# Soft pauses for a background modulation stream, and the FFN's right columns first, in a two-layer diffusion trunk

## The chip, the cores and the metric

The kernel runs on one core of a Trainium2 chip, in one launch. The metric is the device time of that launch in microseconds (us). Engines are named as in the profile: PE (TensorE's matmuls) and PEld (its weight loads), DVE (VectorE), ACT (ScalarE), POOL (GpSimd) and SP (SyncE, which here only issues transfers).

## The reference, cut to what matters

Two layers with the same structure run over 640 tokens of width 1024: 128 context tokens and 512 latent tokens, each group with its own condition vector. Only the last part of a layer and its modulation matter here.

```python
def trunk_layer(x, cond, p, ctx):
    mod = jax.nn.silu(cond) @ p['w_mod'] + p['b_mod']          # 1024 -> 6 x 1024, fp32
    sh1, sc1, g1, sh2, sc2, g2 = [m[:, None, :] for m in jnp.split(mod, 6, axis=-1)]
    h = rms_norm(x, p['g_attn']) * (1 + sc1) + sh1
    a, new_ctx = mixer_sublayer(h, p, ctx)    # projection, three mixers, three branch products with gates, output product
    x = x + g1 * a
    h = rms_norm(x, p['g_ffn']) * (1 + sc2) + sh2
    x = x + g2 * conv_ffn(h, p)               # up 1024 -> 2 x 2816, width-3 convolution over tokens, a * silu(g), down
    return x, new_ctx
```

The modulation of a layer needs only the condition vectors, so layer 1's can be worked out at any time before layer 1 begins.

## The kernel before, in words

**The planner.** The kernel is written as Python generators ("streams"), and class Order interleaves them while the program is built. A stream yields the things that it waits for; `one` (L355) takes the first stream, by priority number, whose things are all there at the planner's own estimate of PE's time, and if none is, the one that is ready soonest. Each step then puts its instructions behind those already issued on their engines. On the chip nothing is reordered: each engine works through its list. Evacuations, weight preparation and factors have priority 0, most helpers 1, and the main stream, which issues the large products, 2. `later(ns)` (L324) is an event at PE's time plus ns; a stream that waits for it paces itself.

**Slots.** Nearly all intermediate tiles come from one pool of 49 slots in SBUF (tile `u`, NU = 49), which lends four more to the mixer. A stream that needs a slot waits until another gives one back. A second pool (`wb`) holds staged weights and their split halves.

**Products.** Weights and activations are split into a high and a low part, so a product with a 128x128 weight block is three matmuls (`mm3`, `product`). `proj_halves` (L692) makes the 640 columns as two halves of 320, each in a PSUM bank, one after the other, and waits for the activation's chunks two at a time. `proj_whole` (L708) makes both halves chunk by chunk in two banks.

**The FFN.** `ffn_steps` (L82) writes out the main stream's order. Two chunks of 128 hidden channels go in the plain way ("raw", tile `up`); they work on unnormalised input, so they can run while the norm is worked out. The other 20 are made by a seven-product scheme over halves of the depth and of the columns, a chunk being a `Pair` with the PSUM tiles pair_x, pair_y and pair_w. Its steps are "12" (products with B11 and B21), "67" (T2, T3), "54" (T1, T4) and "3" (B22). B11 and B21 are the right half of the columns of the normalised input; all others need the left half too. `modulate_factors` (L1006) makes the normalised, modulated input (tile `hv`) and starts `factors` (L931), which splits it and its sums into seven factors (tiles `f`, `f_hi`, `f_lo`) for each of four depth blocks: 28 slots that live through the whole FFN. Five parts of three to five chunks each are followed by eight down products (tile `dn`), woven between the later chunks; the activations of a part (`a_hi`, `a_lo`, two slots a chunk) are given back after its eighth.

**The modulation.** `Mod.rest` (L782) takes five slots, four of them a ring for weights and one for sums. It makes 1024 modulation values, a vector, in eight k-steps; a k-step loads two 256 KB transfers through SP's queue (tile `mod`) and has four small fp32 matmuls of 128x32 by 128x256, which work in four column groups of the array at once and are eight records in the profile. Two k-steps form a turn. Layer 0's last four vectors run early in the kernel with a pause of 4000 ns between turns. For layer 1's six vectors `next_mod` (L2285) waits for the event `calm`, which is set when layer 0's last branch product (tile `bb`) begins; it then has priority 3, behind the main stream, and no pause. `hurry` (L2292) waits for the FFN's first down product of part 1 (event `rush`), gives it priority 1 with a pause of 2000 ns.

Of the kernel before, what the change touches and what calls it, by code (L numbers as in the profile page):

```python
# [9 lines left out]
F32 = mybir.dt.float32  # L10
# [71 lines left out]
def ffn_steps():  # L82
# [5 lines left out]
    for n in range(NRAW, NFF + 1):  # L88
        up, last = n < NFF, n > NRAW
        weave += [("12", n)] * up + [("54", n - 1)] * last + [("67", n)] * up + [("3", n - 1)] * last  # L90
# [104 lines left out]
class Event:  # L195
    time = INF

# [67 lines left out]
class Order:  # L265
# [58 lines left out]
    def later(self, ns):  # L324

        return self.moment(self.at["PE"] + ns)

    def start(self, gen, prio):
        self.seq += 1
        self.streams.append([prio, self.seq, gen, ()])  # L330
        self.streams.sort(key=lambda s: s[:2])

    def lift(self, gen, prio):
        for s in self.streams:
            if s[2] is gen:
                s[0] = prio
        self.streams.sort(key=lambda s: s[:2])
# [17 lines left out]
    def one(self):  # L355
        now, best, at = self.at["PE"], None, INF
        for s in self.streams:
            r = max((self.ready(x) for x in s[3]), default=0.0)
            if r <= now:
                best = s  # L360
                break
            if r < at:
                best, at = s, r
# [15 lines left out]
def kernel(ctx: ExitStack, tc: tile.TileContext, I, O, depth=2):  # L379
# [360 lines left out]
    class Mod:  # L740
        def __init__(self, l, pc=None, ready=None):
            self.l, self.pc, self.ready, self.pause = l, pc, ready, 0.0 if l else 4000.0
# [39 lines left out]
        def rest(self, vectors, after, whole):  # L782
# [17 lines left out]
            for i in range(0, len(todo), 2):  # L800
                v, k0 = todo[i]
                yield ring[0] + ring[1] + [cT, od.later(self.pause)]
# [4 lines left out]
                for j in range(2):  # L807
                    for g in range(4):
                        mm(acc[32 * g:32 * g + 32, :256], cT[:, k0 + j, :], ring[j][g // 2][:, g % 2 * 256:g % 2 * 256 + 256],
                           k0 + j == a, k0 + j == b, tile_position=(0, 32 * g))  # L810
                if not whole or k0 == KC - 2:
# [6 lines left out]
                for j in range(2):  # L818
                    if i + 2 + j < len(todo):
                        yield [od.until(ring[j][1].ap)]  # L820
                        fetch(i + 2 + j)
                if k0 == KC - 2:
                    yield from self.finish(ms, (v * D,), 256, D)
# [107 lines left out]
    def factors(fa, fb, out, k):  # L931

        L, R = slice(0, HT), slice(HT, NT)
        h1, l1, h2, l2 = yield from ub.several("f_12", 4, 0, F32R)
        b11, b12, b21, b22 = fa[:, R], fa[:, L], fb[:, R], fb[:, L]

        def lo(nm, x, h, l):
            tt(l, x, h.bitcast(F32), SUB, sooner(HT))
            out[nm][k] = (h, l)
            out[nm].ready[k].time = od.known[l.tensor.name]  # L940

        yield [fa]
        act(h1[:, L], b11)
        yield [fb]
        act(h1[:, R], b21)
        act(h2[:, L], b22)
        yield [h1]
        lo("B11", b11, h1[:, L], l1[:, L])
        lo("B21", b21, h1[:, R], l1[:, R])
# [3 lines left out]
        yield [fb]  # L953
        tt(b22, b22, b12, SUB)
        tt(b12, b12, b11, SUB)
        tt(b11, b22, b11, ADD)
        tt(b21, b21, b11, SUB)
        yield [fa]
        act(h2[:, R], b12)
        h3 = yield from U("f_hi", F32R)  # L960
        act(h3[:, L], b11)
        yield [h2]
        lo("T1", b12, h2[:, R], l2[:, R])
        l3 = yield from U("f_lo", F32R)
        yield [h3]
        lo("T2", b11, h3[:, L], l3[:, L])
        act(h3[:, R], b21)
        h4 = yield from U("f_34", F32R)
        act(h4[:, L], b22)
        yield [h3]  # L970
        lo("T4", b21, h3[:, R], l3[:, R])
        yield [h4]
        lo("T3", b22, h4[:, L], h4[:, R])
        out.keep += [h1, l1, h2, l2, h3, l3, h4]
# [1146 lines left out]
    def ffn(l, x, raws, h, pc, mod, ss, nxt, nraws, rush):  # L2121
# [14 lines left out]
        for step in ffn_steps():  # L2136
# [13 lines left out]
            elif kind == "dn":  # L2150
                part, o = i, step[2]
                b0, nb = FFN_PARTS[part]
                if part == 1:
                    rush.time = 0.0
# [5 lines left out]
                yield from proj_halves(w, a, nb, finish(o, part), "dn")  # L2160
# [55 lines left out]
    def program():  # L2216
# [20 lines left out]
        for l in range(depth):  # L2237
# [5 lines left out]
            if l == 0:  # L2243
                od.start(mod.rest((2, 3, 4, 5), mod.have[3], False), 1)
# [3 lines left out]
            lazy = next_mod(nxt, calm)  # L2248
            od.start(lazy, 3)
# [27 lines left out]
            rush = Event()  # L2277
# [86 lines left out]
```

## Time and profile before

| | before |
|---|---|
| median of 3 runs (lowest, highest) | 2235.13 us (2232.56, 2236.04) |
| the profiled execution's own time | 2225.76 us |
| its span, first to last instruction | 2224.0 us |
| PE busy in the span | 2113.6 us (95%) |
| PEld, DVE, ACT, POOL busy | 1978.6, 1561.9, 1122.2, 212.6 us |
| mean granted TensorE clock | 0.989 |

The profiled execution is 9.37 us (0.42%) below the median of the runs. Times inside the trace are counted from the start of its span. Layer 0's FFN begins with the first `up` product at 646 us, layer 1's at 1767 us. A matmul's record is longer than the distance to the next one, since they are pipelined: a run of plain 128x320 matmuls at full clock starts one every 0.147 us or so, each being shown with about 0.31 us.

### The profile page before, as it was taken

The numbers are of one execution on the slowest core, as the hardware profiler recorded it, in microseconds if no ns is written. First come the engines' busy times: TensorE is split into PE (matmuls) and PEld (weight loads), VectorE is DVE, ScalarE is ACT, GpSimd is POOL, SyncE is SP. The second block draws the span as 40 slices with busy tenths as digits, with TensorE's granted clock in tenths as the row PEclk, the third lists the DMA queues.
The fourth block names the chain that finished last, engine by engine and source line by source line (L and its number), as shares of the span: only waits on it lengthen the run. The fifth ranks groups of instructions, "written<-read, shape, count | busy, mean of one in ns | idle before, by whom it ended". The sixth has DMA issues, their size and how long they took to land. (4 is left out here: it accounts for less than half of the span.)

```text
span 2224.0 us, 40076 instructions
## 1 busy us (share of the span) xinstructions
PE 2113.6 (95%) x16208; PEld 1978.6 (89%) x16208; DVE 1561.9 (70%) x2827; ACT 1122.2 (50%) x2063; POOL 212.6 (10%) x283
## 2 busy tenths in 40 slices
PE   6999999999998968999999999999999989999999
PEld 4878988899997826999998989888999988999999
DVE  5376679673579804978777876787745798687785
ACT  4355755553356402544556667455532575445452
POOL 0201010000120001010010110100001200100101
PEclk9999999999999989999999999999999999999999
DMA  9752221112324373222223112211114212232212
GB/s 307 258 182 76 69 64 50 39 48 69 112 81 152 112 246 107 90 78 94 77 65 133 62 54 70 72 51 39 39 57 133 76 39 68 76 98 71 95 65 91
DMA packets 85874, 209.33 MB, mean 94 GB/s; under 512 B 9590, under 2 KB 22518, under 8 KB 85688
## 3 DMA queue, kind: packets, MB, share of 16 engines
q1 hardware_dynamic: 84472, 204.66, 28.7%
q8 instruction: 128, 2.10, 0.4%
q0 software_dynamic: 1216, 2.10, 0.3%
q14 instruction: 58, 0.48, 0.1%
HBM read 197.81 MB, written 10.98 MB: 94 GB/s over the span
## 5 line engine op out<-in xcount | busy, mean ns | idle before, releaser
L454 ACT ACTIVATE w_h<-w_st 128x1024 fp32r<-128x1024 f32 (+4 forms) x292 | 273.7, 940 | 220.0 <-PE dn L445 57.5
L470 DVE TENSOR_TENSOR w_h<-w_st,w_h 128x1024 fp32r<-128x1024 f32 (+4 forms) x253 | 276.7, 1095 | 140.1 <-ACT w_h L454 133.9
L445 PE MATMUL dn<-a_hi,w_h 128*128 128x320 f32 x1408 | 321.4, 310 | 1.1 <-ACT a_hi L454 1.1
L445 PE MATMUL pair_x<-f,w_h 128*128 128x320 f32 x1440 | 230.1, 311 | 11.1 <-ACT f L454 5.7
L445 PEld LDWEIGHTS dn<-a_hi,w_h 128*128 128x128 f32 x1408 | 239.4, 189 | 1.3 <-ACT a_hi L454 1.3
L445 PEld LDWEIGHTS pair_x<-f,w_h 128*128 128x128 f32 x1440 | 216.1, 189 | 14.1 <-ACT f L454 5.9
L445 PE MATMUL dn<-a_lo,w_h 128*128 128x320 f32 x704 | 218.4, 310 | 2.6 <-DVE a_lo L470 2.6
L445 PEld LDWEIGHTS dn<-a_lo,w_h 128*128 128x128 f32 x704 | 133.2, 189 | 2.8 <-DVE a_lo L470 2.8
L482 DVE SCALAR_TENSOR_TENSOR x<-dn,modT,x 128x128 f32<-128x128 f32 (+2 forms) x240 | 97.2, 434 | 54.4 <-PE dn L445 54.1
L445 PE MATMUL gc<-h_hi,w_h 128*128 128x320 f32 x512 | 131.8, 324 | 2.1 <-ACT mg L454 2.1
L445 PE MATMUL ga<-h_hi,w_h 128*128 128x320 f32 x512 | 125.9, 316 | 0.0
L473 POOL TENSOR_TENSOR w_h<-w_st,w_h 128x1024 fp32r<-128x1024 f32 (+3 forms) x39 | 78.3, 2008 | 470.8 <-ACT w_h L454 308.4
L445 PE MATMUL gb<-h_hi,w_h 128*128 128x320 f32 x512 | 119.0, 312 | 0.0
L445 PE MATMUL wo<-m_hi,w_h 128*128 128x320 f32 x768 | 113.0, 309 | 0.0
L445 PEld LDWEIGHTS wo<-m_hi,w_h 128*128 128x128 f32 x768 | 112.8, 188 | 0.0
L445 PE MATMUL mod<-mod,cT 128*32 128x256 f32 x640 | 76.0, 412 | 31.1 <-DMA mod<-in_w_mod_dram 29.8
L445 PEld LDWEIGHTS gc<-h_hi,w_h 128*128 128x128 f32 x512 | 89.0, 189 | 9.5 <-ACT mg L454 3.1
L445 PEld LDWEIGHTS mod<-mod,cT 128*32 128x32 f32 x640 | 21.1, 111 | 78.2 <-DMA mod<-in_w_mod_dram 65.2
L445 PEld LDWEIGHTS ga<-h_hi,w_h 128*128 128x128 f32 x512 | 88.1, 188 | 2.4 <-issue 2.4
L454 ACT ACT_TABLE_LOAD x64 | 82.1, 1283 | 16.0 <-PE hss L445 11.1
L445 PEld LDWEIGHTS gb<-h_hi,w_h 128*128 128x128 f32 x512 | 86.8, 188 | 1.6 <-issue 1.4
L445 PE MATMUL pair_x<-f_hi,w_h 128*128 128x320 f32 x320 | 79.3, 316 | 5.7 <-ACT up_a L454 5.7
(414 smaller groups left out, 5350.4 us busy)
## 6 DMA issues: line engine op xcount, KB each, us to landing
w_st<-in_wt_dram SPq DMA_DIRECT2D x204, 512.0 KB, 3.4
mod<-in_w_mod_dram SPq DMA_DIRECT2D x160, 256.0 KB, 3.8
w_st<-in_wt_dram SPq DMA_DIRECT2D x48, 320.0 KB, 3.0
mod_w<-in_w_mod_dram SPq DMA_DIRECT2D x32, 256.0 KB, 6.4
xd<-x SPq DMA_DIRECT2D x16, 320.0 KB, 6.0
x<-xd SPq DMA_DIRECT2D x16, 320.0 KB, 3.2
w_st<-in_wt_dram SPq DMA_DIRECT2D x16, 256.0 KB
w_st<-in_wt_dram SPq DMA_DIRECT2D x16, 192.0 KB, 2.5
```

The costliest lines, as they stand in the source:

```text
L445: nc.tensor.matmul(out, lhsT, rhs, start=start, stop=stop, **kw)
L454: r = nc.scalar.activation(out=out, in_=in_, func=f, **kw)
L470: nc.vector.tensor_tensor(out, a, b, op=op)
L473: nc.gpsimd.tensor_tensor(out, a, b, op=op)
L482: nc.vector.scalar_tensor_tensor(out=out, in0=a, scalar=s, in1=b, op0=op0, op1=op1)
```

## The change

Three things change.

- **Soft pauses.** A pause becomes an event of a class of its own, `Soft`. `one` looks twice: with all events, and, if no stream is ready, once more without the soft ones. A pausing modulation stream is then taken although its pause is not over. `lift` and `hurry` are gone.
- **Layer 1's modulation** starts at the same event `calm`, but with priority 1 and a soft pause of 3000 ns, and a turn is one k-step, not two. Layer 0's last four vectors keep 4000 ns and two k-steps, softly.
- **The FFN.** The right columns of all eight depth blocks are normalised first and B11 and B21 made of them (`right_factors`), then the left columns and the other five factors (`left_factors`); all eight `hv` slots are held in between. The step "12" of the second chunk pair comes before "67" of the first. The first down product of each part is made by `proj_whole`.

```diff
     weave = []
-    for n in range(NRAW, NFF + 1):
-        up, last = n < NFF, n > NRAW
+    a, b = NRAW, NRAW + 1
+    weave += [("12", a), ("12", b), ("67", a), ("54", a), ("67", b), ("3", a)]
+    for n in range(NRAW + 2, NFF + 1):
+        up, last = n < NFF, True
         weave += [("12", n)] * up + [("54", n - 1)] * last + [("67", n)] * up + [("3", n - 1)] * last
...
+class Soft(Event):
+    pass
...
-    def later(self, ns):
-        return self.moment(self.at["PE"] + ns)
+    def later(self, ns, kind=Event):
+        e = kind()
+        e.time = self.at["PE"] + ns
+        return e
...
     def one(self):
-        now, best, at = self.at["PE"], None, INF
-        for s in self.streams:
-            r = max((self.ready(x) for x in s[3]), default=0.0)
-            if r <= now:
-                best = s
-                break
-            if r < at:
-                best, at = s, r
+        now = self.at["PE"]
+        for kinds in ((), Soft):
+            best, at = None, INF
+            for s in self.streams:
+                r = max((self.ready(x) for x in s[3] if not isinstance(x, kinds)), default=0.0)
+                if r <= now:
+                    return self.step(s)
+                if r < at:
+                    best, at = s, r
...
-        def rest(self, vectors, after, whole):
...
-            for i in range(0, len(todo), 2):
+            n = 1 if whole else 2
+            for i in range(0, len(todo), n):
                 v, k0 = todo[i]
-                yield ring[0] + ring[1] + [cT, od.later(self.pause)]
+                yield [t for j in range(n) for t in ring[(i + j) % 2]] + [cT, od.later(pause, Soft)]
                 if k0 == 0 or not whole:
...
-                for j in range(2):
+                for k in range(k0, k0 + n):
                     for g in range(4):
-                        mm(acc[32 * g:32 * g + 32, :256], cT[:, k0 + j, :], ring[j][g // 2][:, g % 2 * 256:g % 2 * 256 + 256],
-                           k0 + j == a, k0 + j == b, tile_position=(0, 32 * g))
+                        mm(acc[32 * g:32 * g + 32, :256], cT[:, k, :],
+                           ring[(i + k - k0) % 2][g // 2][:, g % 2 * 256:g % 2 * 256 + 256], k == a, k == b,
+                           tile_position=(0, 32 * g))
...
-    def factors(fa, fb, out, k):
-        L, R = slice(0, HT), slice(HT, NT)
-        h1, l1, h2, l2 = yield from ub.several("f_12", 4, 0, F32R)
+    L, R = slice(0, HT), slice(HT, NT)
+    def factor_lo(out, k, nm, x, h, l):
+        tt(l, x, h.bitcast(F32), SUB, sooner(HT))
+        out[nm][k] = (h, l)
+        out[nm].ready[k].time = od.known[l.tensor.name]
+    def right_factors(fa, fb, out, k):
+        h, l = yield from ub.several("f_12", 2, 0, F32R)
+        for nm, x, c in (("B11", fa, L), ("B21", fb, R)):
+            yield [x]
+            act(h[:, c], x[:, R])
+            yield [h]
+            factor_lo(out, k, nm, x[:, R], h[:, c], l[:, c])
+        out.keep += [h, l]
+    def left_factors(fa, fb, out, k):
         b11, b12, b21, b22 = fa[:, R], fa[:, L], fb[:, R], fb[:, L]
-        def lo(nm, x, h, l):
-            tt(l, x, h.bitcast(F32), SUB, sooner(HT))
-            out[nm][k] = (h, l)
-            out[nm].ready[k].time = od.known[l.tensor.name]
-        yield [fa]
-        act(h1[:, L], b11)
+        lo = lambda nm, x, h, l: factor_lo(out, k, nm, x, h, l)
+        h2, l2 = yield from ub.several("f_12", 2, 0, F32R)
         yield [fb]
-        act(h1[:, R], b21)
         act(h2[:, L], b22)
-        yield [h1]
-        lo("B11", b11, h1[:, L], l1[:, L])
-        lo("B21", b21, h1[:, R], l1[:, R])
         yield [h2]
         lo("B22", b22, h2[:, L], l2[:, L])
-        yield [fb]
+        yield [fa, fb, out["B11"].ready[k], out["B21"].ready[k]]
         tt(b22, b22, b12, SUB)
+        h4 = yield from U("f_34", F32R)
+        act(h4[:, L], b22)
         tt(b12, b12, b11, SUB)
         tt(b11, b22, b11, ADD)
-        tt(b21, b21, b11, SUB)
-        yield [fa]
-        act(h2[:, R], b12)
         h3 = yield from U("f_hi", F32R)
         act(h3[:, L], b11)
+        tt(b21, b21, b11, SUB)
+        l3 = yield from U("f_lo", F32R)
+        yield [h4]
+        lo("T3", b22, h4[:, L], h4[:, R])
+        yield [h3]
+        lo("T2", b11, h3[:, L], l3[:, L])
+        act(h2[:, R], b12)
+        act(h3[:, R], b21)
         yield [h2]
         lo("T1", b12, h2[:, R], l2[:, R])
-        l3 = yield from U("f_lo", F32R)
-        yield [h3]
-        lo("T2", b11, h3[:, L], l3[:, L])
-        act(h3[:, R], b21)
-        h4 = yield from U("f_34", F32R)
-        act(h4[:, L], b22)
         yield [h3]
         lo("T4", b21, h3[:, R], l3[:, R])
-        yield [h4]
-        lo("T3", b22, h4[:, L], h4[:, R])
-        out.keep += [h1, l1, h2, l2, h3, l3, h4]
+        out.keep += [h2, l2, h3, l3, h4]
...
     def modulate_factors(x, r, mod, i, offs, out):
         gsc, sh = mod.gsc[:, i], mod.T[:, 24 * i:24 * i + 8]
-        cols = [(slice(a, a + n), slice(offs[e], offs[e] + n), e) for e, (a, n) in enumerate(((0, NP), (NP, NS)))]
-        for k in range(KC // 2):
-            f = []
-            for kk in (k, k + KC // 2):
-                yield [r, mod.have[12 * i + 4 + kk // 2], mod.have[12 * i + kk // 2]]
-                v = yield from U("hv")
-                eng = sooner(NT)
-                for c, o, e in cols:
-                    tt(v[:, c], x[kk][:, c], r[:, o], MUL, eng)
-                yield [v]
-                for c, _, e in cols:
-                    act(v[:, c], v[:, c], AF.Identity, scale=gsc[:, kk, e:e + 1], bias=sh[:, kk, e:e + 1])
-                f.append(v)
-                del v
-            od.start(factors(f[0], f[1], out, k), 0)
-            del f
+        n = HT - NP
+        sides = (((slice(HT, NT), slice(offs[1] + n, offs[1] + NS), 1),),
+                 ((slice(0, NP), slice(offs[0], offs[0] + NP), 0), (slice(NP, HT), slice(offs[1], offs[1] + n), 1)))
+        v = [None] * KC
+        for cols, then in zip(sides, (right_factors, left_factors)):
+            for k in range(KC // 2):
+                for kk in (k, k + KC // 2):
+                    yield [r, mod.have[12 * i + 4 + kk // 2], mod.have[12 * i + kk // 2]]
+                    if v[kk] is None:
+                        v[kk] = yield from U("hv")
+                    eng = sooner(HT)
+                    for c, o, e in cols:
+                        tt(v[kk][:, c], x[kk][:, c], r[:, o], MUL, eng)
+                    yield [v[kk]]
+                    for c, _, e in cols:
+                        act(v[kk][:, c], v[kk][:, c], AF.Identity, scale=gsc[:, kk, e:e + 1], bias=sh[:, kk, e:e + 1])
+                od.start(then(v[k], v[k + KC // 2], out, k), 0)
+                if then is left_factors:
...
-                if part == 1:
-                    rush.time = 0.0
...
-                yield from proj_halves(w, a, nb, finish(o, part), "dn")
+                if o:
+                    yield from proj_halves(w, a, nb, finish(o, part), "dn")
+                else:
+                    ps, ev = (yield from proj_whole(w, a, nb, HT, "dn")), finish(o, part)
+                    for hf in range(2):
+                        od.start(ev(hf, ps.pop(0)), 0)
+                    del ps, ev
...
-                od.start(mod.rest((2, 3, 4, 5), mod.have[3], False), 1)
+                od.start(mod.rest((2, 3, 4, 5), mod.have[3], 4000.0, False), 1)
...
-            lazy = next_mod(nxt, calm)
-            od.start(lazy, 3)
+            od.start(next_mod(nxt, calm), 1)
...
-                od.start(hurry(nxt, lazy, rush), 1)
...
-            yield from nxt.rest(range(6), after, True)
+            yield from nxt.rest(range(6), after, 3000.0, True)
...
-    def hurry(mod, lazy, when):
-        yield [when]
-        mod.pause = 2000.0
-        od.lift(lazy, 1)
```

## Rows read from the trace of the kernel before

**Rows 1.** The page: PE's busy time, PE in 40 slices, GB/s in the slices
```profile
PE 2113.6 (95%) x16208; PEld 1978.6 (89%) x16208; DVE 1561.9 (70%) x2827; ACT 1122.2 (50%) x2063; POOL 212.6 (10%) x283
...
PE   6999999999998968999999999999999989999999
...
GB/s 307 258 182 76 69 64 50 39 48 69 112 81 152 112 246 107 90 78 94 77 65 133 62 54 70 72 51 39 39 57 133 76 39 68 76 98 71 95 65 91
```

**Rows 2.** Windows: stretch, length, busy of engines, clock, DMA share, GB/s
```profile
540.00:590.00 50.00, 50.00 (x343) 50.00 (x342) 28.36 (x40) 16.37 (x23) 6.18 (x4) 1.00 0.39 114
...
782.00:856.00 74.00, 47.11 (x291) 12.33 (x290) 3.55 (x24) 3.06 (x7) 3.57 (x5) 0.91 0.74 235
...
1797.00:1812.00 15.00, 6.11 (x26) 5.50 (x25) 14.51 (x30) 8.22 (x16) 0.20 (x2) 0.68 0.00 0
1812.00:1872.00 60.00, 55.11 (x363) 53.59 (x363) 58.83 (x99) 39.09 (x67) 0.41 (x4) 0.98 0.27 88
```

**Rows 3.** Timeline of PE: start, us, what, idle before with its releaser
```profile
782.68 1.07 PE L445 MATMUL mod<-mod,cT 128*32 128x256 f32 x16
...
855.48 0.42 PE L445 MATMUL pair_x<-f_hi,w_h 128*128 128x320 f32 x1 [0.70 <-ACT up_a L454]
```

**Rows 4.** Waits, 640 to 900: us in total, times, longest
```profile
POOL up_a L2069 <- PE mod L445: 72.9, 1, 72.9
...
PE mod L445 <- DMA mod<-in_w_mod_dram: 27.8, 39, 2.3
```

**Rows 5.** Timeline of SP's issues; tile mod's transfers, 640 to 900; tile bb
```profile
655.00 0.43 SPq L510 DMA_DIRECT2D pc<-in_prm_dram  x1
...
670.67 21.21 SPq L510 DMA_DIRECT2D mod<-in_w_mod_dram  x20
...
710.16 1.96 SPq L510 DMA_DIRECT2D mod<-in_w_mod_dram  x4
...
L510 SPq DMA_DIRECT2D mod<-in_w_mod_dram x96: 327/328/1172, 670.7 to 850.1; - x96
...
L445 PE MATMUL bb<-ob_hi,w_h x256: 302/309/313, 540.7 to 1710.8; 128*128 128x320 f32 x128
```

**Rows 6.** Timeline of PE: first pair in layer 0 and in layer 1
```profile
675.95 1.50 PE L445 MATMUL pair_x<-f,w_h 128*128 128x320 f32 x9
...
691.44 0.71 PE L445 MATMUL pair_x<-f,w_h 128*128 128x320 f32 x3
...
1796.79 1.48 PE L445 MATMUL pair_x<-f,w_h 128*128 128x320 f32 x9
1803.92 0.63 PE L445 MATMUL pair_x<-f,w_h 128*128 128x320 f32 x1 [5.65 <-ACT f L454]
1807.79 0.90 PE L445 MATMUL pair_x<-f,w_h 128*128 128x320 f32 x2 [3.24 <-DVE f L470]
...
1898.83 0.31 PE L445 MATMUL pair_x<-f_hi,w_h 128*128 128x320 f32 x1
```

**Rows 7.** Timeline of PE: modulation between other matmuls in layer 0
```profile
64.25 2.92 PE L445 MATMUL mod<-mod,cT 128*32 128x256 f32 x16 [1.98 <-DMA mod<-in_w_mod_dram]
...
82.87 0.30 PE L445 MATMUL rc<-h_hi,w_h 128*128 128x320 f32 x1
83.10 1.07 PE L445 MATMUL mod<-mod,cT 128*32 128x256 f32 x16
84.10 0.41 PE L445 MATMUL rc<-h_hi,w_h 128*128 128x320 f32 x1
...
85.09 0.38 PE L450 MATMUL modt<-cn,mod 128*128 128x128 f32 x2
```

**Rows 8.** DVE's groups, 1775 to 1815, shapes apart: busy, mean ns
```profile
L470 DVE TENSOR_TENSOR f<-hv,f 128x320 fp32r<-128x320 f32 x19 | 8.6, 487 | 0.0
...
L470 DVE TENSOR_TENSOR hv<-x,rstd 128x512 f32<-128x512 f32 x7 | 4.8, 685 | 0.2 <-ACT rstd L454 0.2
...
L470 DVE TENSOR_TENSOR hv<-x,rstd 128x128 f32<-128x128 f32 x7 | 2.3, 329 | 3.7 <-ACT rstd L454 3.7
```

**Rows 9.** Timeline of PE: first down product in layer 1
```profile
1868.52 0.41 PE L445 MATMUL dn<-a_hi,w_h 128*128 128x320 f32 x1 [1.05 <-ACT a_hi L454]
1871.54 0.63 PE L445 MATMUL dn<-a_lo,w_h 128*128 128x320 f32 x1 [2.61 <-DVE a_lo L470]
```

More of the change, by code (lines that the diff above doesn't have):

```diff
@@ L330, in start @@
         self.streams.append([prio, self.seq, gen, ()])
-        self.streams.sort(key=lambda s: s[:2])
-    def lift(self, gen, prio):
-        for s in self.streams:
-            if s[2] is gen:
-                s[0] = prio
         self.streams.sort(key=lambda s: s[:2])
@@ L355, in one @@
     def one(self):
-        now, best, at = self.at["PE"], None, INF
-        for s in self.streams:
-            r = max((self.ready(x) for x in s[3]), default=0.0)
-            if r <= now:
-                best = s
-                break
-            if r < at:
-                best, at = s, r
+        now = self.at["PE"]
[7 more added lines that the diff above has]
+                    best, at = s, r
         if best is None:
@@ L741, in __init__ @@
         def __init__(self, l, pc=None, ready=None):
-            self.l, self.pc, self.ready, self.pause = l, pc, ready, 0.0 if l else 4000.0
+            self.l, self.pc, self.ready = l, pc, ready
             self.T = prm.tile([P, 48, 2], F32, tag="modT", bufs=2, name=f"modT{l}")
@@ L780, in first, with rest @@
             yield from self.finish(ms, pieces, P, 256)
-        def rest(self, vectors, after, whole):
+        def rest(self, vectors, after, pause, whole):
             yield [after]
@@ L806, in rest @@
                 a, b = (0, KC - 1) if whole else (k0, k0 + 1)
-                for j in range(2):
+                for k in range(k0, k0 + n):
                     for g in range(4):
-                        mm(acc[32 * g:32 * g + 32, :256], cT[:, k0 + j, :], ring[j][g // 2][:, g % 2 * 256:g % 2 * 256 + 256],
-                           k0 + j == a, k0 + j == b, tile_position=(0, 32 * g))
-                if not whole or k0 == KC - 2:
+                        mm(acc[32 * g:32 * g + 32, :256], cT[:, k, :],
+                           ring[(i + k - k0) % 2][g // 2][:, g % 2 * 256:g % 2 * 256 + 256], k == a, k == b,
+                           tile_position=(0, 32 * g))
+                end = k0 + n == KC
+                if end or not whole:
                     yield [acc]
@@ L817, in rest @@
                     del acc
[L818 to L822, printed above, removed]
+                for j in range(i, i + n):
+                    if j + 2 < len(todo):
+                        yield [od.until(ring[j % 2][1].ap)]
+                        fetch(j + 2)
+                if end:
                     yield from self.finish(ms, (v * D,), 256, D)
@@ L1007, in modulate_factors @@
         gsc, sh = mod.gsc[:, i], mod.T[:, 24 * i:24 * i + 8]
-        cols = [(slice(a, a + n), slice(offs[e], offs[e] + n), e) for e, (a, n) in enumerate(((0, NP), (NP, NS)))]
-        for k in range(KC // 2):
-            f = []
-            for kk in (k, k + KC // 2):
-                yield [r, mod.have[12 * i + 4 + kk // 2], mod.have[12 * i + kk // 2]]
-                v = yield from U("hv")
-                eng = sooner(NT)
-                for c, o, e in cols:
-                    tt(v[:, c], x[kk][:, c], r[:, o], MUL, eng)
-                yield [v]
-                for c, _, e in cols:
-                    act(v[:, c], v[:, c], AF.Identity, scale=gsc[:, kk, e:e + 1], bias=sh[:, kk, e:e + 1])
-                f.append(v)
-                del v
-            od.start(factors(f[0], f[1], out, k), 0)
-            del f
+        n = HT - NP
[16 more added lines that the diff above has]
+                if then is left_factors:
+                    v[k] = v[k + KC // 2] = None
     def scaled(x, k, ready, mod, i, gh, gl, done):
@@ L2119, in pair_split, with ffn @@
         yield from keep_split(i, z, ah, al, have)
-    def ffn(l, x, raws, h, pc, mod, ss, nxt, nraws, rush):
+    def ffn(l, x, raws, h, pc, mod, ss, nxt, nraws):
         ah, al = {}, {}
@@ L2276, in program @@
                 ss = nraws = None
-            rush = Event()
-            if nxt is not None:
-                od.start(hurry(nxt, lazy, rush), 1)
-            yield from ffn(l, x, raws, h, pc, mod, ss, nxt, nraws, rush)
+            yield from ffn(l, x, raws, h, pc, mod, ss, nxt, nraws)
             raws = nraws
```

## The prediction

> **What bounds the kernel now.** I read the page first: PE is busy for 95% of the span, but two of its 40 slices, the 14th and 15th, fall to 8 or 6, and the 15th, in the middle of the kernel, moves 246 GB/s, which otherwise only the opening does [rows 1]. So PE's order is the bound, and one place in it is odd. Windows put it at 782 to 856 us: 74 us in which DVE and ACT do 3.6 and 3.1 us of work, at a granted clock of 0.91 [rows 2]. PE's timeline shows what is there: modulation matmuls from 782.68 on, and the next FFN matmul at 855.48, 72.8 us later [rows 3]. In the waits one entry of 72.9 us stands out: POOL's first write to a new `up_a` tile waits for PE's modulation. `up_a` and the modulation's tiles come from the same slots, so the FFN waits for a slot, and the slot is one that the modulation gives back when all its vectors are done [rows 4]. That is the reading on which all rests. The slots agree: 28 factors, 10 for the five chunks of a part, four for two chunks more, six for two pairs at work, one or two for weights make 49 or 50 of 49, without the modulation's five.
>
> Why the modulation is still there at 782 is in SP's timeline. Its stream could start at 540.7, with the first `bb` matmul, but was first served at 655.00 (the parameter load that it begins with), since with priority 3 it moves only when the main stream has nothing. Of its 96 transfers 32 are out before the block: 20 from 670.67, and three groups of four like that at 710.16 [rows 5]. The other 64, 32 of 48 k-steps, fall into the block, where a k-step takes 72.8 / 32 = 2.27 us because each waits for its load (39 waits, 27.8 us, with a few before the block [rows 4]).
>
> Layer 1's FFN has no modulation beside it, so it is the measure for layer 0's. From the first pair matmul to the one that follows the fourth down product it takes 1898.83 - 1796.79 = 102.0 us; in layer 0 the same stretch takes 855.48 - 675.95 = 179.5 us [rows 3, 6]. The difference, 77.5 us, is what layer 1's modulation costs now.
>
> **The change part by part.**
>
> *Priority 1 from `calm` on.* The stream starts at about 541. One turn lasts the 3.0 us pause, its own k-step, and half a piece of the main stream (six matmuls at 1.50 - 0.31 over eight, 0.149 us each [rows 6], so 0.45): some 4.0 us, 48 of them 193 us, which ends near 734. The first pair matmul, at 676 before, is then pushed back by some 40 k-steps, to about 699, and the old block, 107 us behind it, would come at 806. The modulation ends some 70 us ahead of the point where the slots run out; even at half the pace in the FFN it would be ahead.
>
> What a k-step costs in the dense stretch is read in layer 0, where turns stand between other matmuls: from the `rc` matmul at 82.87 to the next at 84.10 are 1.23 us, and without the turn 0.15, so two k-steps cost 1.08 [rows 7]. In a turn of one, only the gap ahead of it (83.10 less 83.02) is not halved: 0.08 + 0.50 = 0.58 us. 48 of them are 27.8 us. The six pairs of transposes take at most 0.38 each by their record, which overlaps both neighbours; I take 0.2, so 1.2. Together +29.0.
>
> The Trainium skill, page "TensorEngine Tiling (Array Packing)", section Key Properties, says that a change of the tiling mode drains TensorE; one k-step a turn doubles the changes, which speaks against this edit. It gives no price. If the whole 1.08 us of a turn were such changes, the sum would be 48 x 1.08 = 52 instead of 28, and the time 24 us later than forecast. The trace is nearer to 0.58: the gap that it shows ahead of a turn is 0.08 us.
>
> The transfers: 512 KB every 4.0 us are 131 GB/s on top of 114 where the branch products run [rows 2], 245 in all; the opening slice moved 307 and the block 235 [rows 1, 2]. A ring half is refilled two turns, 8 us, ahead of its use; a k-step at the block's pace needs 2.27. So I cost waits for loads at nothing in the dense stretch. The cover is gone if SP's queue stops for longer than that.
>
> *Soft pauses.* They matter only where the planner has nothing for PE. In layer 1's FFN entry, and so in layer 0's with no modulation waiting, PE is idle for 5.65 + 3.24 = 8.9 us [rows 6]; at 2.27 us that holds four k-steps, whose 4 x 0.58 = 2.3 us are then free. For layer 0's last four vectors I take zero: from minus 2.0 (the one wait of 1.98 us at 64.25 gone [rows 7]) to plus 4 (two more like it).
>
> *Right columns first.* It removes the 8.9 us in which "12" waits for B11 of the last depth block. But DVE is what is late there: 14.5 of 15 and 58.8 of 60 us busy from 1797 to 1872 [rows 2], up to the wait of the first down product for `a_lo`, from DVE again [rows 9]. The reorder gives DVE no less to do. It splits the 512 columns of a multiplication: 0.487 + 0.39 instead of 0.685 (between the 320 and the 128 wide rows [rows 8]), +0.19 us for each of eight, +1.5 a layer. PE reaches "67" earlier and waits there for T2 and T3, which need the left columns. From below: minus 8.9 a layer if it all holds, and another 2 if the clock, granted at 0.68 from 1797 to 1812 between its two levels of 1.2 and 2.4 GHz [rows 2], stays up. From above: plus 6 in layer 0, since eight `hv` tiles are now held together with the plain chunks' 16 slots and the modulation's five, so the left factors may wait for slots while DVE idles. DVE's busy rows are the nearest; I take minus 2 in layer 1 and plus 3 in layer 0, +1.
>
> *First down product with both halves.* While the last chunk's `a_lo` is missing, PE has four chunks of both halves to do, 24 matmuls instead of 12: 12 x 0.147 = 1.8 us less of the 1.05 + 2.61 us wait [rows 9]. The other parts' first products show no wait. Two layers: -3.5. It takes two PSUM banks at once of six; at that step I count at most four in use, so no cost.
>
> **The sum.** 2225.76 (the profiled execution) - 77.5 + 29.0 - 2.3 + 1 - 3.5 = 2172.5 us. The runs' median lies 9.4 us above the profiled execution; I find nothing in the change that touches that and add it: 2182 us.
>
> **The rivals.**
>
> *Slots run out sooner.* The modulation may still hold its five slots when the FFN's tiles want them: two pairs are opened together now, and `hv` is held longer. Then the k-steps that are left run alone, at 2.27 instead of 0.58 us. With the nine to twenty that I expect to be left at the FFN's entry this is +15 to +34, so 2197 to 2216. For it: by my count the slots are 46 to 49 of 49 there. Against it: before, the modulation held the same five through the first 106 us of that FFN, and only then did all stop.
>
> *Loads stall PE.* Slower than before: priority 1 puts each k-step into PE's list whether or not the planner's load time is right, and everything behind it waits. The place is 541 to 734, the price the wait of one k-step, and it decides from (77.5 - 29.0 + 4.8) / 48 = 1.1 us per k-step on. At the longest wait of before, 2.3 us [rows 4], the time is 2182 + 48 x 2.3 = 2292. For it: SP's queue is in order, and weight loads stand in it that wait for buffers. Against it: the mean of before's 39 waits is 0.71 us, and those were taken with no other work between the loads; at 0.71 the time would be 2216, still faster.
>
> *The entry really closes.* DVE may defer weight work that is needed later, and both layers gain the 8.9 and the clock: 2182 - 1 - 2 x 10.9 = 2159.
>
> **How the numbers follow.** The forecast has 0.66 (its own range 2170 to 2194, from the entry's bounds, +6 to -9, and the +4 of layer 0's vectors), slots 0.16, loads slower than before 0.06, the entry closing 0.12. The range 2162 to 2210 leaves out the loads, a third of the slots' case and half of the last, 2 in 10. Faster by over 0.2% (4.5 us, about what a measurement of this kernel can tell from no change) in all but the loads' case and a sliver of 0.01 beside it: 0.93; same 0.01, slower 0.06.
>
> **What would show it.** Right: the slice with 246 GB/s is gone and some 130 GB/s more lie from 541 to about 734; no wait of `up_a` for modulation over 5 us; modulation in PE's timeline as eight records between `bb`, `gb` and `wo` matmuls, costing under 0.65 us each; layer 0's stretch of 179.5 us near 100; PE's wait in the first pair at T2 or T3 and no longer at B11. Wrong: a stretch with modulation alone on PE, waits for its loads of over a microsecond among `wo` matmuls, or an FFN entry in layer 0 that is longer than 102 us by more than 10.

## The result and the profile after

| | before | after |
|---|---|---|
| median of 4 runs (lowest, highest) | 2234.09 us (2232.56, 2236.04) | 2173.62 us (2171.07, 2179.26) |
| profiled execution, span | 2225.76, 2224.0 us | 2171.07, 2169.2 us |
| mean granted TensorE clock | 0.989 | 0.992 |

The ratio is 0.9732 (95% interval 0.9709 to 0.9756): 60 us faster, where 53 were forecast (2182 us, range 2162 to 2210).

The page of the changed kernel, PE's busy time, PE in 40 slices and GB/s, answers [rows 1]:
```profile
PE 2090.6 (96%) x16208; PEld 1970.0 (91%) x16208; DVE 1563.8 (72%) x2844; ACT 1124.7 (52%) x2079; POOL 215.3 (10%) x282
...
PE   6999999999999999999999999999999989999999
...
GB/s 306 261 184 92 58 68 61 30 50 69 212 201 165 156 88 73 93 80 67 75 84 127 62 57 61 65 51 40 40 71 115 78 40 95 72 88 76 90 64 93
```
The 6 in the 15th slice is gone, and so is its 246 GB/s; 212, 201, 165 and 156 stand in the 11th to the 14th, from 542 us on. PE's timeline shows what moves there and where it ends:
```profile
544.26 0.64 PE L449 MATMUL mod<-mod,cT 128*32 128x256 f32 x8
...
548.56 0.64 PE L449 MATMUL mod<-mod,cT 128*32 128x256 f32 x8
...
704.55 0.60 PE L449 MATMUL pair_x<-f,w_h 128*128 128x320 f32 x3
...
752.53 0.64 PE L449 MATMUL mod<-mod,cT 128*32 128x256 f32 x8
...
802.42 0.31 PE L449 MATMUL pair_x<-f_hi,w_h 128*128 128x320 f32 x1
```
One k-step (eight records) every 4.30 us from the first branch product on, 36 ahead of the first pair matmul and 12 behind it, the last at 752.53. The stretch from the first pair matmul to the one after the fourth down product takes 802.42 - 704.55 = 97.9 us instead of 179.5 [rows 3, 6]. In PE's own waits from 540 to 704 nothing stands, and of PE's 40 waits for tile `mod`'s loads one of 2.3 us is left, in layer 0's early part.

In layer 1's entry, where no modulation runs, PE's timeline and the windows answer [rows 6, 2]:
```profile
1744.86 1.92 PE L449 MATMUL pair_x<-f,w_h 128*128 128x320 f32 x12
...
1753.87 0.41 PE L449 MATMUL pair_x<-f_hi,w_h 128*128 128x320 f32 x1 [1.81 <-ACT up_a L458]
...
1756.25 0.63 PE L449 MATMUL pair_x<-f_lo,w_h 128*128 128x320 f32 x1 [1.52 <-DVE f_lo L474]
...
1759.94 0.64 PE L449 MATMUL pair_x<-f_hi,w_h 128*128 128x320 f32 x1 [1.98 <-ACT f_hi L458]
1763.90 0.64 PE L449 MATMUL pair_x<-f_lo,w_h 128*128 128x320 f32 x1 [3.33 <-DVE f_lo L474]
...
1769.48 2.04 PE L449 MATMUL pair_x<-f,w_h 128*128 128x320 f32 x12 [1.48 <-ACT up_g L458]
...
1821.04 0.41 PE L449 MATMUL dn<-a_lo,w_h 128*128 128x320 f32 x1 [2.15 <-DVE a_lo L474]
...
1843.85 0.31 PE L449 MATMUL pair_x<-f_hi,w_h 128*128 128x320 f32 x1
```
```profile
1745.00:1760.00 15.00, 9.69 (x59) 8.72 (x57) 14.62 (x31) 10.21 (x25) 1.33 (x5) 0.83 0.19 70
1760.00:1820.00 60.00, 53.45 (x340) 51.64 (x340) 59.39 (x101) 40.09 (x69) 0.84 (x8) 0.93 0.21 70
```
The first twelve matmuls run through: no wait at B11 any more. The idle time comes back a few microseconds later, at T2. It begins 7.2 us behind the first pair matmul, where it began 1.5 us behind it before, and its four waits, for `up_a`, `f_lo`, `f_hi` and `f_lo`, are 1.81 + 1.52 + 1.98 + 3.33 = 8.6 us where 8.9 stood. A fifth, 1.48 us for `up_g`, was 0.29 us before, so PE idles in this entry for 10.1 us instead of 9.2. DVE is busy for 14.6 of 15 and 59.4 of 60 us, as before. The stretch takes 98.99 us instead of 102.04; the wait at the first down product is 2.2 us instead of 3.7 [rows 9].

By stages, in the two profiled executions:

| stage | before | after | difference |
|---|---|---|---|
| first `bb` to first pair matmul, layer 0 | 135.3 | 163.9 | +28.6 |
| layer 0's stretch to the fourth down product | 179.5 | 97.9 | -81.7 |
| from there to layer 1's first pair matmul | 941.3 | 942.4 | +1.1 |
| layer 1's stretch | 102.0 | 99.0 | -3.1 |
| the rest | 865.8 | 866.0 | +0.2 |
| span | 2224.0 | 2169.2 | -54.8 |

### The profile page after: what moved, and what is told of

Read it like the earlier page. It is cut to its first block, busy times and chain, and to the rows that moved or that the text cites. A ratio compares the mean times of both kernels' runs of the same rounds, so it can differ in the third digit from the quotient of the medians.

```text
span 2169.2 us, 40095 instructions
## 1 busy us (share of the span) xinstructions
PE 2090.6 (96%) x16208; PEld 1970.0 (91%) x16208; DVE 1563.8 (72%) x2844; ACT 1124.7 (52%) x2079; POOL 215.3 (10%) x282
## 5 line engine op out<-in xcount | busy, mean ns | idle before, releaser
L477 POOL TENSOR_TENSOR w_h<-w_st,w_h 128x1024 fp32r<-128x1024 f32 (+2 forms) x43 | 88.8, 2065 | 500.3 <-ACT w_h L458 341.9
L449 PE MATMUL wo<-m_hi,w_h 128*128 128x320 f32 x768 | 117.5, 311 | 0.0
L486 DVE SCALAR_TENSOR_TENSOR cv_a<-up_g,pc,cv_a 128x641 f32<-128x641 f32 x80 | 72.2, 903 | 12.6 <-ACT cv_a L458 11.0
L486 DVE SCALAR_TENSOR_TENSOR up_g<-up_a,pc,up_g 128x641 f32<-128x641 f32 x80 | 70.8, 885 | 13.9 <-ACT up_g L458 11.6
```

The lines of the kernel that those rows point to most:

```text
L449: nc.tensor.matmul(out, lhsT, rhs, start=start, stop=stop, **kw)
L477: nc.gpsimd.tensor_tensor(out, a, b, op=op)
L486: nc.vector.scalar_tensor_tensor(out=out, in0=a, scalar=s, in1=b, op0=op0, op1=op1)
```

## The experiments

Theory: the FFN stood because the modulation still held its five slots, and the gain is that it ends in time. Rivals: the FFN's own order brings a good part; softness does.

**The modulation's part alone.** All FFN edits undone; the diff, against the changed kernel, shows a line of each.
```diff
-    weave += [("12", a), ("12", b), ("67", a), ("54", a), ("67", b), ("3", a)]
...
+    for n in range(NRAW, NFF + 1):
...
-                od.start(then(v[k], v[k + KC // 2], out, k), 0)
...
+            od.start(factors(f[0], f[1], out, k), 0)
...
-                if o:
...
+                yield from proj_halves(w, a, nb, finish(o, part), "dn")
```


> The changed kernel with the FFN as before: old order of the steps, factors of both column halves together, every down product in two halves after each other. Soft pauses and the new start of layer 1's modulation stay. Theory (the gain is the end of the block in which the FFN stood without slots): nearly all of the gain is here, the span is 2172 to 2178 us against 2169.2 with the whole change; layer 1's stretch from the first pair matmul to the one after the fourth down product is 102 us as before, layer 0's below 105. Rival (a good part of the gain comes from the FFN's new order): the span is above 2185.

Measured: 2185.26 us (ratio to before 0.9782, 0.9759 to 0.9804), span 2183.8: four fifths of the gain, but 12 us less than the whole change. Layer 1's stretch is 100.9 us; layer 0's is 110.1 and not 97.9. So neither theory nor rival as I put them. PE's timeline shows where the 12 us are:
```profile
707.84 1.58 PE L446 MATMUL mod<-mod,cT 128*32 128x256 f32 x16
711.51 1.41 PE L446 MATMUL mod<-mod,cT 128*32 128x256 f32 x8 [2.08 <-DMA mod<-in_w_mod_dram]
...
724.91 1.60 PE L446 MATMUL mod<-mod,cT 128*32 128x256 f32 x8 [0.68 <-DMA mod<-in_w_mod_dram]
726.43 0.71 PE L446 MATMUL pair_x<-f,w_h 128*128 128x320 f32 x3
```
In the old FFN order the planner sees the hole at B11, skips the soft pause and puts nine k-steps into it. On the chip their loads are late, and the pair's last group waits behind them until 726.43, 20.0 us after the first, where layer 1 without modulation has the first matmul of that group at 7.1 and the others at 11.0 [rows 6]. The hole is filled with something longer than itself.

**The FFN's part alone**, on the kernel before: the same lines the other way round.

> The kernel before with only the FFN's edits: right columns first, the new order of the steps, first down product with both halves. The modulation keeps priority 3 and its late lift. Theory: the block of modulation alone on PE is still there, 55 to 75 us long, layer 1's stretch is 99 us, and the span is 2212 to 2224 us against 2224.0. Rival: below 2205.

Measured: 2238.77 us, ratio 1.0027 (1.0011 to 1.0042), 0.3% slower than before, and the span of 2235.5 us is above the 2212 to 2224 of the theory. PE's timeline again shows the block:
```profile
783.56 1.07 PE L448 MATMUL mod<-mod,cT 128*32 128x256 f32 x16
...
871.41 0.42 PE L448 MATMUL pair_x<-f_hi,w_h 128*128 128x320 f32 x1 [0.70 <-ACT up_a L457]
```
It is 87.9 us long, above the 55 to 75 that I expected: without the hole at B11 fewer k-steps run early, 8 instead of 14, so that 76 transfers are left for the block instead of 64. By PE's records 40 k-steps run in it, where before had 34, the first two of them with loads issued earlier: 87.9 / 40 = 2.20 us each, and 72.8 / 34 = 2.14 before. So the price of a k-step in the block is nearly the same. Layer 1's stretch is 98.95 us, the 3 us of the FFN's edits.

**A later modulation.** Is it the slots? One number is changed.
```diff
-            yield from nxt.rest(range(6), after, 3000.0, True)
+            yield from nxt.rest(range(6), after, 8000.0, True)
```


> The changed kernel with a pause of 8000 instead of 3000 ns for layer 1's modulation, so that it is late and still holds its five slots when the FFN of layer 0 needs them. Theory (slots): a block comes back at the same place in the FFN, some 105 us behind the first pair matmul, with 11 to 21 k-steps alone on PE at about 2.3 us each, and the span is 2190 to 2215 us. Rival (the block was a matter of priority and pauses, and soft pauses alone prevent it): no stretch of over 5 us with modulation alone, span within 5 us of 2169.

Measured: 2202.65 us, span 2201.4. The block is back, with high priority and soft pauses in place:
```profile
688.04 1.93 PE L449 MATMUL pair_x<-f,w_h 128*128 128x320 f32 x12
...
790.68 1.07 PE L449 MATMUL mod<-mod,cT 128*32 128x256 f32 x16
...
832.46 0.64 PE L449 MATMUL pair_x<-f_hi,w_h 128*128 128x320 f32 x1 [0.70 <-ACT up_a L458]
```
It begins 102.6 us behind the first pair matmul, after the fourth down product like that of before (106.7), lasts 41.8 us and holds 18 k-steps by PE's records, 2.32 us each. In its waits POOL's first write to `up_a` waits 44.2 us for modulation:
```profile
POOL up_a L2084 <- PE mod L449: 44.2, 1, 44.2
```
That speaks for the slots and against priority alone: the modulation has the same priority as in the changed kernel and the FFN stops at the same point. No run gives the pool more slots; that the resource is the slots rests on the tile that this wait names.

**Two k-steps to a turn**, pause 6000 ns.
```diff
-            n = 1 if whole else 2
+            n = 2
```


> The changed kernel with two k-steps to a turn for layer 1's modulation as well, and a pause of 6000 ns, so that the rate stays. In the changed kernel a turn of one k-step sets PE back by 0.77 us (4.30 us from turn to turn, of which 24 matmuls take 3.52), in layer 0 a turn of two by 1.18. Theory (0.36 us of each turn is for the turn, 0.41 for each k-step): the first pair matmul of layer 0's FFN comes 5 to 7 us earlier than at 704.6, and the span is 2161 to 2166 us. Rival (the price is that of the k-steps): the first pair matmul within 2 us of 704.6, the span within 3 us of 2169.

Measured: 2172.81 us (0.9724, 0.9700 to 0.9748), span 2171.6: no different. Counted from the first `bb` matmul, the first pair matmul comes 161.8 us later with 40 k-steps ahead of it, where the changed kernel has 163.9 with 36: 2.1 us earlier, not 5 to 7. A pair of transposes sets the changed kernel's `bb` matmuls back by 0.23 us (from 576.63 to 577.15 us, less two steps of 0.147). With that, (161.8 - 135.3 - 5 x 0.23) / 20 = 1.27 us a turn of two against (28.6 - 4 x 0.23) / 36 = 0.77 for a turn of one: about 0.27 us is for the turn and 0.50 for each k-step. So the price of a turn is there, but the 2.1 us are lost again in layer 0's stretch, 100.2 us with 8 k-steps in it; two waits for loads, 1.88 and 0.67 us, stand there.

**Pauses that are never skipped**, with the old FFN order and with the new one.
```diff
-                yield [t for j in range(n) for t in ring[(i + j) % 2]] + [cT, od.later(pause, Soft)]
+                yield [t for j in range(n) for t in ring[(i + j) % 2]] + [cT, od.later(pause)]
```


> As the first experiment (FFN as before, layer 1's modulation early with priority 1 and a pause of 3000 ns), but with pauses that are never skipped. Theory (in the first experiment the planner filled the hole of layer 0's FFN entry, where PE waits for B11, with k-steps whose loads were not there, and these held the pair's matmuls up on PE): the pair's fourth matmul group comes 10 to 14 us after the first pair matmul and not 20, layer 0's stretch falls from 110 to 100 to 104 us, and the span is some 6 to 10 us under the 2183.8 of the first experiment. Rival (the new order of the FFN itself gave those 12 us of layer 0): the stretch stays within 3 us of 110.

> The changed kernel with pauses that are never skipped. Theory: in the changed kernel PE's list has hardly a hole between layer 0's branch and FFN, so skipping a pause matters little: layer 0's stretch within 3 us of 97.9, the span within 4 us of 2169. Rival (the soft pauses give part of the gain by filling holes): the last modulation matmul comes over 20 us after 752 and the span is above 2175.

Measured with the old order: 2172.32 us (0.9714, 0.9690 to 0.9738), the whole gain with none of the FFN's edits. Its profiled execution was the slowest of four (span 2173.9), yet layer 0's stretch is 98.1 us. PE's timeline at the hole:
```profile
709.03 1.07 PE L446 MATMUL mod<-mod,cT 128*32 128x256 f32 x16
712.80 1.29 PE L446 MATMUL mod<-mod,cT 128*32 128x256 f32 x8 [2.70 <-DMA mod<-in_w_mod_dram]
...
717.56 1.05 PE L446 MATMUL pair_x<-f,w_h 128*128 128x320 f32 x3
```
Four k-steps instead of nine, and the last group of the pair comes 9.9 us after the first. With the new order: 2174.32 us (0.9729, 0.9710 to 0.9748), span 2173.6, just outside the 4 us of its theory, stretches of 100.2 and 99.0 us. So softness costs 12 us in the old order and nothing that can be measured in the new one.

**The first down product in two halves again**, one execution.
```diff
-                if o:
-                    yield from proj_halves(w, a, nb, finish(o, part), "dn")
-                else:
...
+                yield from proj_halves(w, a, nb, finish(o, part), "dn")
```


> The changed kernel with every first down product made in two halves after each other again. Theory: in layer 1 PE's waits for the last chunk's a_hi and a_lo grow from 2.2 us by 1.8, layer 1's stretch goes from 99.0 to 100 to 101 us. Rival (it does nothing, since DVE sets the end of the stretch anyway and the second half fills no wait): 99.0 within 0.5.

Measured: layer 1's stretch 103.5 us, and PE's two waits there:
```profile
1747.93 1.93 PE L449 MATMUL pair_x<-f,w_h 128*128 128x320 f32 x12
...
1822.32 0.42 PE L449 MATMUL dn<-a_hi,w_h 128*128 128x320 f32 x1 [0.94 <-ACT a_hi L458]
...
1825.34 0.42 PE L449 MATMUL dn<-a_lo,w_h 128*128 128x320 f32 x1 [2.60 <-DVE a_lo L474]
...
1851.45 0.31 PE L449 MATMUL pair_x<-f_hi,w_h 128*128 128x320 f32 x1
```
3.5 us instead of 2.2, in the direction of the theory. The stretch grew by 4.5 us, more than the 1.8 us of matmuls. Counted from the first pair matmul, the wait for `a_lo` ends at 77.4 us instead of 76.2, and what follows takes 26.1 us instead of 22.8, at a granted clock of 0.93 instead of 1.00. So beside the matmuls 1.2 us stand ahead of the wait and 1.5 behind it, the latter with the clock; this is one execution.

**The kernel before once more**, one execution.

> The kernel before, a second profile. The first profiled execution (2225.76 us) lies 9 us under the median of its runs. Theory A (the loads of the block run slower in most executions): layer 0's stretch is longer than 179.5 us by most of the difference, all other stretches are equal. Theory B (the granted clock is lower in other places too): the difference is spread over the span, with a lower mean clock.

Measured: span 2232.2, 8.2 us more than in the first profile. Layer 0's stretch takes 185.5 us, 5.9 more, at the same number of transfers in the block (64). The windows of the stretch (granted clock third from the end):
```profile
676.00:782.00 106.00, 94.67 (x637) 83.40 (x637) 88.49 (x159) 56.96 (x98) 2.59 (x10) 0.94 0.40 130
782.00:880.00 98.00, 71.90 (x440) 34.69 (x439) 15.98 (x45) 10.64 (x20) 9.35 (x10) 0.88 0.61 190
```
In the first profile the clock was 0.98 and 0.93 in these windows. So theory A in the main, with a lower clock in the same place; the rest is +1.3 ahead of it, +1.9 behind it and -1.1 in layer 1's stretch.

**The right columns alone undone**, one execution: the first two pieces of the first diff; soft pauses and the down product stay.

> The changed kernel with the factors of both column halves together and the old order of the steps; the first down product with both halves and the soft pauses stay. Theory (with soft pauses the hole at B11 is filled with k-steps whose loads are late): layer 0's stretch is 108 to 111 us and not 97.9, with the loads' waits between the first and the last group of the first pair product; in layer 1, with no modulation, it is 99 to 101. Rival (the down product was what shortened layer 0's stretch): below 102 in layer 0.

Measured: 106.2 us in layer 0's stretch and 98.6 in layer 1's, span 2178.7. As in the first experiment layer 0's hole is filled with nine k-steps, most of which wait for loads; a little less than expected. In layer 1 PE's timeline has the old wait at B11 in full:
```profile
1755.01 1.49 PE L446 MATMUL pair_x<-f,w_h 128*128 128x320 f32 x9
1761.90 0.64 PE L446 MATMUL pair_x<-f,w_h 128*128 128x320 f32 x1 [5.41 <-ACT f L455]
1765.78 0.90 PE L446 MATMUL pair_x<-f,w_h 128*128 128x320 f32 x2 [3.24 <-DVE f L471]
...
1829.18 0.41 PE L446 MATMUL dn<-a_lo,w_h 128*128 128x320 f32 x1 [2.14 <-DVE a_lo L471]
...
1853.57 0.31 PE L446 MATMUL pair_x<-f_hi,w_h 128*128 128x320 f32 x1
```
Yet the stretch is as short as the changed kernel's, 98.6 us against 99.0. Set beside the others, with the stretch cut where PE's wait for `a_lo` ends, this says what each edit does in layer 1 (one execution each):

| layer 1's stretch | first pair matmul to the end of the wait, us | from there to the stretch's end, us | granted clock there |
|---|---|---|---|
| before | 74.8 | 27.3 | 0.89 |
| right columns first, down product in halves | 77.4 | 26.1 | 0.93 |
| old factors, both halves of the down product | 74.2 | 24.4 | 0.93 |
| changed kernel | 76.2 | 22.8 | 1.00 |

The right columns make the first part longer, and the down product makes the second shorter. Up to that wait DVE is busy for 73.1 of 74.8 us before and for 75.2 of 76.2 after: its work sets the moment.

**Slower ahead of the FFN, faster in it**, in three forms: one k-step to a turn, 4500 then 1500 ns from the FFN's first step; two k-steps, 9000 then 3000; and the latter with the fast pause only from the first pair product on.
```diff
...
+            if nxt is not None:
+                nxt.pause = 1500.0
             yield from ffn(l, x, raws, h, pc, mod, ss, nxt, nraws)
```
The third form has these two lines at the step "12" instead, with 3000.

> The changed kernel with layer 1's modulation slower before layer 0's FFN (pause 4500 ns) and faster in it (1500 ns from the FFN's first step on). Theory (PE's time in the branch and output products is dear, 0.77 us a k-step, while DVE sets the length of the FFN's first 98 us, so k-steps are free there as long as they end before the slots run out): some 27 instead of 36 k-steps come before the first pair matmul, which is 6 to 8 us earlier; layer 0's stretch stays at 98 to 103 us; the median is 2168 to 2172. Rival (the FFN's stretch has no more room than the 12 k-steps that it holds now): it grows by 6 us or more and the time is that of the changed kernel or worse.

> As the late and fast version, with two k-steps to a turn and pauses of 9000 and 3000 ns, the same rates. Theory (0.27 to 0.36 us of a turn are for the turn itself): against the late and fast version the first pair matmul comes another 3 to 5 us earlier, the median is 2164 to 2170. Rival: as in the turn of two before, what is won ahead of the FFN is lost in it; within 2 us of the late and fast version.

> As the late version with two k-steps to a turn, but the fast pause (3000 ns) begins with the first pair product instead of the first plain up product, so that the fast turns don't fall among the up matmuls. Theory (k-steps among the up matmuls cost their full price, among the pair products of layer 0 they are free): some 26 k-steps instead of 34 come before the first pair matmul, which is 5 to 7 us earlier than at 700.2; layer 0's stretch is 100 to 103 us with 22 k-steps in it; the median is 2163 to 2168. Rival (the stretch is full): it grows by as much as is won before it, the median stays at 2169 to 2172.

| | k-steps ahead | `bb` to first pair | in the stretch | layer 0's stretch | median | ratio to before |
|---|---|---|---|---|---|---|
| changed kernel | 36 | 163.9 | 12 | 97.9 | 2173.62 | 0.9709 to 0.9756 |
| one a turn, late | 33 | 162.7 | 15 | 99.1 | 2171.40 | 0.9707 to 0.9733 |
| two a turn, late | 34 | 159.3 | 14 | 100.4 | 2170.21 | 0.9700 to 0.9727 |
| two a turn, fast from the pairs on | 26 | 151.4 | 22 | 104.7 | 2168.72 | 0.9697 to 0.9728 |

The first form missed its aim: the fast pause began among the plain up products, so 33 and not 27 k-steps came ahead. The third shows both sides: 12.5 us won ahead of the stretch, 6.8 given back in it. Up to some 15 k-steps in the stretch cost next to nothing, 22 cost 104.7 - 97.9 over 10, about 0.7 us for each further one. The medians fall in order, but the intervals overlap; a further gain, 12.5 - 6.8 = 5.7 us, is read from the stages of one execution each, whose spans differ by 3.0 us. Neither of the last two forms reached the median that I expected (2164 to 2170 and 2163 to 2168). The second also lies within 2 us of the first, as its rival said, and the third's stretch is above the 100 to 103 us of its theory.

## Why the prediction was right, and where not

*The block.* Right, with its cause: it is gone, and it comes back at the same place when the modulation is late, with `up_a` waiting for modulation. The 2.27 us of a k-step in it count the 32 whose loads are issued there; by PE's records it holds 34 of 2.14 us, and that price nearly held in two other kernels (2.20 and 2.32). Of the page, one reading was off: the row of slices has its 6 in the 15th, but its 8s in the 13th and the 16th, not in the 14th; the windows read next, 782 to 856 us, lie in the 15th and the 16th, so nothing hangs on it. The slots' rival is that case; the changed kernel ended its modulation at 752.5, 50 us ahead of the point where the FFN had stopped.

*The dense k-step.* Mis-sized: 0.77 us, not 0.58. I halved all of a turn but the gap ahead of it. The turn of two in layer 0 also delays the matmul after it (84.10 to 84.35 us, 0.25 instead of 0.15), and the runs give 0.27 us to each turn. The stage ahead of the FFN grew by 28.6 us where 36 x 0.58 + 4 x 0.2 = 21.7 were to be expected. With the rule of the Trainium skill, page "TensorEngine Tiling (Array Packing)", section Key Properties, that a change of mode drains TensorE, the runs agree in sign (0.27 us a turn); the 1.08 us that I set as its bound was too high.

*The free k-steps.* Mis-sized the other way: I took four as free, and the twelve in layer 0's stretch were all free, since that stretch is even shorter than layer 1's without any (97.9 and 99.0 us). In layer 1's PE idles for 12.9 us, in layer 0's for 3.9: twelve k-steps of 0.77 us fill the rest. I had divided the idle time by 2.27 us, the price of a k-step that waits for its loads. 8 x 0.58 = 4.6 us less than forecast.

*Right columns first.* The wait moved from B11 to T2, as forecast, but the gain of 2 us in layer 1 did not show: the edit costs there. PE's wait for `a_lo` ends 74.2 to 75.0 us behind the first pair matmul in the five executions with the old factors and 76.1 to 77.4 us in the nine with the right columns first, about 1.4 us later. That is near the +1.5 us that I counted for DVE's split operations; what I set against it did not come. What I did not see either is what the edit is worth beside the soft pauses: it removes the hole into which they would put k-steps with late loads. Together the two cost nothing, soft pauses without it 12 us. With pauses that are never skipped, layer 0's stretch is no shorter with the FFN's edits than without (100.2 and 98.1 us). My +3 us for layer 0's slots did not show.

*First down product with both halves.* All that layer 1 won lies behind that wait, 22.8 us instead of 27.3. The 1.8 us of matmuls that I forecast are in it (24.4 us against 26.1 at the same clock, 0.93). The rest, which I had not counted, goes with the clock. In five executions with both halves together the granted clock is 1.00 there and the part takes 22.8 to 22.9 us; in the other four of this kind it is 0.93 and the part takes 24.4 to 24.5. In all five with the halves one after the other it is 0.89 to 0.94, for 25.9 to 27.3 us. Why it falls in some executions and not in others is open. So layer 1's 3.1 us agree with the 3.8 of my sum, but not part by part.

*Soft pauses.* I costed them at a gain of 2.3 us, the four free k-steps. The k-steps were free, but not because pauses are skipped: with pauses that are never skipped twelve lie in the stretch as well. No run shows a gain of softness.

*The sum.* The cause and the direction were right; that 2172.5 us was forecast for the profiled execution and 2171.07 measured is luck, since errors cancel. The stage ahead of the first pair matmul took 6.9 us more than forecast. Layer 0's stretch took 10 us less: 102.0 + 3 - 1.8 + 8 x 0.58 = 107.8 was its part of the sum, and 97.9 was measured. Of that 4.6 us are the free k-steps and 3 the slots; the other 2.4 us are about what the stretch varies by (97.9, 99.4 and 100.2 us in three kernels with twelve k-steps in it and the right columns first). The miss of the median, 8 us, is the step "I find nothing in the change that touches that": 5.9 of the 8.2 us between the two profiles of the kernel before lie in the stretch with the block, so most of the 9.4 us probably went with it. After the change the median lies 2.6 us above the profiled execution.

*The signs.* Right: the slice with 246 GB/s, the eight records among `bb`, `gb` and `wo`, the stretch near 100, the wait at T2. Wrong: a k-step under 0.65 us, and "no wait of `up_a` for modulation over 5 us". POOL has one of 15.3:
```profile
POOL up_a L2084 <- PE mod L449: 19.0, 2, 15.3
```
It is a slot handed over just the same, but PE had work meanwhile, so that wait alone tells nothing; the hole on PE does. The rival of loads that stall PE did not come about among the branch products (no wait there), but it did in the old FFN order with soft pauses, where I had not looked for it.

## What to carry to other kernels

A background stream that holds buffers has a deadline, the point at which the main work needs them; give it a rate that meets it, and check the rate by the moment it ends, not by how little it disturbs. Filling a planner's holes is only a gain if what is filled in is there on the chip as well: transfers that the planner thinks fast make the hole longer. And when an edit moves a wait on an engine that another engine feeds at 97% or more, look for the wait a few microseconds later before counting it as won.

## What the runs showed that I had not expected

- A turn of modulation matmuls in column groups costs about 0.27 us beside its 0.50 us a k-step: 0.77 us for one k-step, 1.27 for two.
- In the hole of the first experiment the same eight records take 1.41 to 1.73 us instead of 0.64. From 712.6 to 726.2 us the granted clock is 0.50 there, the lower of its two levels (1.2 GHz), and the one group of eight that has no wait ahead of it takes 1.08 us (at 716.10). The rest is probably the wait for loads inside the turn.
- Two edits that are worth -50 and +4 us alone are worth -60 together. But with pauses that are never skipped the first alone is worth -61: the second only mends what the soft pauses do.
- In layer 1 the right columns first make DVE's part longer by about 1.4 us; the first down product with both halves is all that gains there.
